# A hybrid encoder block: transfers of V on another queue, another order of the attention minima, and a thinner fourth head pair

## The chip, the cores and the metric

The kernel runs on one core of a Trainium2 chip. The metric is device microseconds of one execution; less is better. Five engines share the work, each with an instruction stream of its own that it takes strictly in order: PE (TensorE, matrix products and transposes), DVE (VectorE), ACT (ScalarE), POOL (GpSimd) and SP (SyncE, which here only issues DMAs). DMAs are also issued from ACT's and POOL's streams. Streams wait for each other by semaphores.

## The reference

One layer over 512 rows of 1024 values, in float32:

```python
h = rms_norm(x, g)
xr, gate, q, k, v = split(h @ w_in)              # 512 each
xr = centred_depthwise_conv(xr)
y_rnn = (rg_lru(xr, forward) + rg_lru(xr, backward)) * gelu(gate)
y_attn = dilated_attention(q, k, v, rel_bias)    # 8 heads of 64
x = x + concat(rms_norm(y_rnn), rms_norm(y_attn)) @ w_out
x = x + square(relu(rms_norm(x) @ w_up)) @ w_down
return rms_norm(x, final_g)
```

The attention has three dilated windows, of which the kernel makes two groups of keys for each block of 128 queries: near ones (within 64 positions, at most 256 keys) and far ones (a multiple of 4 away, hence 128 keys of the same class, position modulo 4).

## The kernel before, in words

Every product is made of three float32r matmuls (`mm3`, L311 to L314): high times high, low times high and high times low part. Weights come in chunks of 128x1024 by DMA into `wraw` (three buffers), or into `tw`, `ws` and `ts` where several blocks are summed first. ACT rounds a chunk to its high part `whi` (`conv_hi`, L260) and DVE subtracts to get the low part `wlo` (`conv_lo`, L268); both happen three chunks ahead of use. After a low part the next `wraw` load is issued on SP's queue (`emit_dma`, L243).

PE, ACT, DVE and POOL run in the order in which the program is written (a manual schedule); for SP the framework chooses the order. So a step's place in the text is its place in each engine's queue.

The part in question runs from 84 to 200 us of the span:

- **V.** ScalarE writes V to the tile `vs` (`v_evac`, L717). Far keys need V sorted by class, so `v_far` (L719 to L722) copies it on-chip into `vc`, the other half of the same tile, by five DMAs on SP's queue. Their first reader is the product of pair 0, in pair 1's turn (`att_av`).
- **The head pairs.** The loop `for i in range(5)`, `for u in range(4)` (L1058) handles heads 2i and 2i+1 together; u is a block of 128 queries. `att_s` (L766) makes the score matmuls: for u = 0 the near scores `pn` of blocks 0 and 1 (L777) and the far scores `pf` of all four (L784), for u = 2 the near scores of blocks 2 and 3. `pn` lies in two PSUM banks that both halves of a pair share. `att_f` (L797) adds the bias to far scores and takes each row's minimum (the scores are negated); `att_e` takes up that minimum, does the same with near scores (L816) and lets ScalarE take the exponential (L819). In the trace a minimum is a custom DVE instruction and a short read of its accumulator, twice, for the two heads.
- One turn later the exponentials are transposed (`att_t`, L831, three groups `a`, `b`, `c` for each head), copied to `ett` by ScalarE, the row factors 1/sum are transposed (`att_r`, L391) and copied to `zrow`, and `att_av` (L912) makes the pair's output `pav`. Transposes, factors and outputs take turns in two PSUM banks (tag `et`), so each needs the copy of the one two before it. DVE multiplies `pav` by `zrow` into `yp` (L928), ScalarE squares it (`ysq`) and scales it (`at`).
- **Fillers.** Between these steps `fill` takes thunks from a queue: first the Q and K projections of the next pairs (48), then the recurrent half of W_out (32 thunks, `pwo`, three matmuls each). `FILL` (L1055) says how many stand at the four places of each (i, u); where it names nothing, one at each. `plan` puts small steps beside them, among them `end(t)` (two DVE products that finish scan t, L570 and L571).
- **W_out's attention half** runs as seven 2x2 block products (Strassen-like, `OSEQ`: 11, s2, s3, s4, 21, s1, 22). The sums of weight blocks s1 to s4 are made by DMA: `load_x` (L992) loads the first block on SP's queue and adds the others on POOL's queue. Each result is added to `x1` by `wo_x` (L1120) with the row factor `rc[1]`: column sums by PE (`col_sums`, L411), mean by DVE (L396), power -1/2 by POOL (L399), and `nrc`, its negative, by DVE (L1147). The next product of the same bank has to wait for that addition.

After 205 us W_up and W_down follow in the same manner, to 530 us, and the final norm.

Of the kernel before, what the change touches and what calls it, by code (L numbers as in the profile page):

```python
# [12 lines left out]
FT = mybir.dt.float32  # L13
FR = mybir.dt.float32r
AF = mybir.ActivationFunctionType
OP = mybir.AluOpType

P = 128
S = 512
# [89 lines left out]
def hybrid_kernel(ctx: ExitStack, tc, xw, xn, w_in, w_v, w_out, w_up, w_dn, gates, vecs, rel, onehot, fg, out):  # L109
    nc = tc.nc  # L110
# [8 lines left out]
    act = nc.scalar.activation  # L119
# [111 lines left out]
    def oblock(b):  # L231
        return w_out[1, int(b[1]) - 1, int(b[0]) - 1]
# [486 lines left out]
    def v_far(j):  # L719
        for a, b, s in (((0, P, 32 * j - 16),) if j else ((0, 64, 112), (64, P, 0))):  # L720
            n = (b - a) // 4
            nc.sync.dma_start(vc[s:s + n], vs[a:b, j, :])  # L722

    last = [scan_ops_end(t) for t in range(4)]

# [266 lines left out]
    def load_x():  # L992
        xb = big.tile([P, KD, S], FT, name="x1", tag="bigA")
        for n in range(2):
            for g in range(4):
                x1[g, n] = xb[:, 2 * g + n, :]
                nc.sync.dma_start(x1[g, n], xn[2 * g + n])
        ws = big.tile([P, 4, 1024], FT, name="ws", tag="bigB")
        for i, (n, bs) in enumerate((("s2", ("11", "12", "22")), ("s3", ("12", "22")), ("s4", ("11", "12", "22", "21")), ("s1", ("11", "12")))):
            t = raws[C_WA + OSEQ.index(n)] = ws[:, i, :]  # L1000
            nc.sync.dma_start(t, oblock(bs[0]))
            for b in bs[1:]:
                nc.gpsimd.dma_start(t, oblock(b), accum_op=OP.add)

    def rnn_end(t):
        last[t]()
# [10 lines left out]
    def end(t):  # L1017
        return lambda: rnn_end(t)

    def sq_(t):  # L1020
        return lambda: rnn_sq(t)
# [4 lines left out]
    def op(fn, *a):  # L1026
        return lambda: fn(*a)


    plan = {(0, 0, 0): [end(0)], (0, 0, 2): [sq_(0), add], (0, 0, 3): [end(1)],  # L1030
            (0, 1, 1): [sq_(1)],
            (0, 2, 3): [add],
            (1, 0, 2): [end(2)],
# [7 lines left out]
    def beside(*key):  # L1041
        for e in plan.pop(key, ()):
            e()
# [5 lines left out]
    for key, fs in (((4, 0, 4), [(o_sum, "s1", 0), (o_sum, "s2", 0), (o_sum, "s3", 0), (o_sum, "s3", 1)]),  # L1049
# [2 lines left out]
                    ((4, 2, 0), [(o_hi, "s3", 0), (o_hi, "s3", 1)]), ((4, 2, 2), [(o_lo, "s3", 0), (o_lo, "s3", 1), (o_sum, "22", 0)]),  # L1052
                    ((4, 2, 4), [(o_hi2, 0)]), ((4, 3, 0), [(o_lo2, 0), (o_hi, "s1", 0)]), ((4, 3, 4), [(o_lo, "s1", 0), (o_hi, "22", 0), (o_lo, "22", 0)])):
        plan[key] = [op(*a) for a in fs]
    FILL = {(3, 1): (1, 1, 1, 0), (3, 2): (1, 1, 1, 0), (3, 3): (1, 1, 1, 0), (4, 0): (0, 1, 0, 0), (4, 1): (0, 1, 0, 1), (4, 2): (0, 1, 0, 0), (4, 3): (0, 0, 0, 1)}  # L1055


    for i in range(5):  # L1058
        for u in range(4):
            if i == 0:  # L1060
                v_far(u)
            if i < 4 and u in (0, 2):
                att_s(i, u)
                if i < 3:
                    load_tw(2 * i + 2 + u // 2)
            if i >= 1 and u < 3:
                att_t(2 * i - 2, "abc"[u])
                att_t(2 * i - 1, "abc"[u])
            if i < 4:
                if u < 2:  # L1070
                    att_f(i, 2 * u)
                    att_f(i, 2 * u + 1)
                att_e(i, u)
            if u == 0 and i >= 1:
                att_z(i - 1)
            beside(i, u, 0)
            fill(FILL.get((i, u), (1, 1, 1, 1))[0])
            beside(i, u, 1)
            fill(FILL.get((i, u), (1, 1, 1, 1))[1])
            if u == 1 and i >= 1:  # L1080
                att_r(i - 1)
            if u == 0 and i >= 2:
                att_y(i - 2)
            beside(i, u, 2)
            fill(FILL.get((i, u), (1, 1, 1, 1))[2])
            beside(i, u, 3)
            fill(FILL.get((i, u), (1, 1, 1, 1))[3])
            beside(i, u, 4)
            if u == 3 and 1 <= i < 4:
                att_av(i - 1)  # L1090
    assert not plan
# [43 lines left out]
    def h2_l(k):  # L1135
        nc.vector.tensor_tensor(hb["l"][:, k, :], hm[k], f(hb["h"])[:, k, :], op=OP.subtract)

    fill(1)
    att_av(3)
    att_y(3)  # L1140
    fill(4)
    cs = col_sums(ssy[1], "gs")
    rc[1] = rstd_cols(cs, S)
    o_sum("s1", 1)
    o_sum("s2", 1)
    nrc = consts.tile([P, 4], FT, name="nrc")
# [563 lines left out]
```

## Time and profile before

| | |
|---|---|
| median of 3 runs | 538.03 us (537.99 to 540.79) |
| the profiled execution | 539.04 us, its span 537.2 us |
| TensorE clock granted | 0.996 |
| PE busy | 524.9 us, 98% of the span |
| DVE, ACT, POOL busy | 423.3, 352.2, 64.0 us |
| DMA | 104.10 MB, 194 GB/s in the mean |

Times inside the profile count from the start of the span. A row of the timeline gives start, duration, engine, line, operation, output and inputs, shape, and in brackets how long the engine had stood idle and what released it. A row of the list of waits gives the total, the count and the longest. A row of the table by stretches gives the stretch, its length, the busy time of PE, PE's weight loads, DVE, ACT and POOL with their instruction counts, the clock, the share of DMA and GB/s. Matmuls are pipelined, so their modelled ends overlap the next starts.

### The profile page before, as it was taken

How to read it: one execution, taken by the hardware profiler on the slowest of the kernel's cores; microseconds unless marked ns; L12 is line 12 of the kernel's file. 1: busy time of each engine (PE TensorE's matmuls, PEld its weight loads, DVE VectorE, ACT ScalarE, POOL GpSimd, SP SyncE). 2: the span in 40 equal slices, each digit the busy share in tenths (PEclk: the TensorE clock that was granted, in tenths of full speed). 3: DMA queues.
4: the chain of work that ended last, by engine and by line, in shares of the span. 5: the costliest groups of instructions: out<-in, count | busy, mean ns of one | idle time of the engine just before them, and what ended most of it. 6: DMA issues, size and time to landing. Idle time of an engine off the chain costs nothing.

```text
span 537.2 us, 9162 instructions
## 1 busy us (share of the span) xinstructions
PE 524.9 (98%) x3507; PEld 448.3 (83%) x3507; DVE 423.3 (79%) x695; ACT 352.2 (66%) x557; POOL 64.0 (12%) x91
## 2 busy tenths in 40 slices
PE   8999999899999999999999999999999999999995
PEld 6866888687887778889999888888999999888884
DVE  6897787776674799889769987879756987987885
ACT  7677957567845745586576755566657686655664
POOL 3330000000001130001030213001001110131000
PEclk9999999999999999999999999999999999999998
DMA  7754068642299688856586799995888496799704
GB/s 276 210 161 141 32 171 182 183 114 70 90 298 307 165 166 203 285 193 180 166 177 177 195 252 274 288 356 116 282 235 206 117 220 193 174 301 263 174 0 157
DMA packets 34587, 104.10 MB, mean 194 GB/s; under 512 B 3981, under 2 KB 6954, under 8 KB 34544
## 3 DMA queue, kind: packets, MB, share of 16 engines
q1 hardware_dynamic: 26304, 74.66, 41.2%
q0 software_dynamic: 7920, 28.61, 28.5%
q8 instruction: 27, 0.44, 0.4%
q10 hardware_dynamic: 320, 0.25, 0.1%
q14 instruction: 16, 0.13, 0.1%
HBM read 96.15 MB, written 4.21 MB: 187 GB/s over the span
## 4 chain that ended last, share of the span: by engine, by line
PE 75%; DMA 10%; ACT 5%; DVE 5%; issue 2%; POOL 1%; SPq 0%; DVEq 0%; ACTq 0%; POOLq 0%
PE pu L314 10%; PE pu L313 10%; PE pu L312 10%; PE pd L312 9%; PE pd L314 9%; PE pd L313 9%; DMA ws<-in_w_out_dram 6%; DMA wraw<-in_w_in_dram 3%; PE pqk L312 2%; PE pqk L313 1%; PE pqk L314 1%; PE pg L502 1%; PE pxr L312 1%; PE pxr L314 1%; PE pxr L313 1%
## 5 line engine op out<-in xcount | busy, mean ns | idle before, releaser
L268 DVE TENSOR_TENSOR wlo<-wraw,whi 128x1024 fp32r<-128x1024 f32 x73 | 88.9, 1221 | 28.3 <-ACT whi L260 28.1
L260 ACT ACTIVATE whi<-wraw 128x1024 fp32r<-128x1024 f32 x70 | 74.0, 1059 | 44.6 <-PE pd L314 20.5
L313 PE MATMUL pd<-wlo,ah 128*128 128x512 f32 (+1 forms) x195 | 75.2, 386 | 0.0
L312 PE MATMUL pd<-whi,ah 128*128 128x512 f32 (+1 forms) x195 | 75.2, 386 | 0.0
L314 PE MATMUL pd<-whi,al 128*128 128x512 f32 (+1 forms) x195 | 75.2, 386 | 0.0
L313 PE MATMUL pu<-hl,whi 128*128 128x256 f32 x224 | 63.4, 283 | 0.0
L314 PE MATMUL pu<-hh,wlo 128*128 128x256 f32 x224 | 63.4, 283 | 0.0
L312 PE MATMUL pu<-hh,whi 128*128 128x256 f32 x224 | 63.4, 283 | 0.0
L260 ACT ACTIVATE whi<-tw 128x1024 fp32r<-128x1024 f32 x36 | 38.1, 1060 | 37.0 <-DMA tw<-in_w_up_dram 10.1
L314 PE MATMUL pu<-h2h,wlo 128*128 128x256 f32 (+1 forms) x200 | 60.1, 301 | 0.2 <-DVE wlo L268 0.2
L312 PE MATMUL pu<-h2h,whi 128*128 128x256 f32 (+1 forms) x200 | 60.1, 300 | 0.0
L313 PE MATMUL pu<-h2l,whi 128*128 128x256 f32 (+1 forms) x200 | 60.0, 300 | 0.0
L268 DVE TENSOR_TENSOR wlo<-tw,whi 128x1024 fp32r<-128x1024 f32 x36 | 44.0, 1222 | 17.5 <-ACT whi L260 17.5
L312 PEld LDWEIGHTS pu<-hh,whi 128*128 128x128 f32 x224 | 43.0, 192 | 0.0
L313 PEld LDWEIGHTS pu<-hl,whi 128*128 128x128 f32 x224 | 43.0, 192 | 0.0
L314 PEld LDWEIGHTS pu<-hh,wlo 128*128 128x128 f32 x224 | 43.0, 192 | 0.0
L314 PEld LDWEIGHTS pd<-whi,al 128*128 128x128 f32 x195 | 36.6, 188 | 7.4
L313 PEld LDWEIGHTS pd<-wlo,ah 128*128 128x128 f32 x195 | 36.6, 188 | 7.4
L312 PEld LDWEIGHTS pd<-whi,ah 128*128 128x128 f32 x195 | 36.6, 188 | 7.2
L260 ACT ACTIVATE whi<-ts 128x1024 fp32r<-128x1024 f32 x24 | 25.5, 1061 | 24.3 <-PE pd L314 18.1
L314 PEld LDWEIGHTS pu<-h2h,wlo 128*128 128x128 f32 x200 | 38.3, 191 | 1.8 <-DVE wlo L268 0.6
L312 PEld LDWEIGHTS pu<-h2h,whi 128*128 128x128 f32 x200 | 38.3, 191 | 1.3
(265 smaller groups left out, 1222.6 us busy)
## 6 DMA issues: line engine op xcount, KB each, us to landing
wraw<-in_w_up_dram SPq DMA_DIRECT2D x25, 512.0 KB
ts<-in_w_dn_dram POOLq DMA_DIRECT2D x24, 512.0 KB, 13.6
wraw<-in_w_dn_dram SPq DMA_DIRECT2D x24, 512.0 KB
tw<-in_w_up_dram SPq DMA_DIRECT2D x15, 512.0 KB
tw<-in_w_up_dram POOLq DMA_DIRECT2D x15, 512.0 KB, 7.4
wraw<-in_w_in_dram SPq DMA_DIRECT2D x13, 512.0 KB
ts<-in_w_dn_dram SPq DMA_DIRECT2D x8, 512.0 KB
tw<-in_w_dn_dram SPq DMA_DIRECT2D x8, 512.0 KB
```

What stands on the lines that cost most here:

```text
L260: act(hi, raws[i], AF.Copy)
L268: nc.vector.tensor_tensor(lo, r, f(splits[i][0]), op=OP.subtract)
L312: nc.tensor.matmul(o, lhsT=a[0], rhs=b[0], start=bool(first), stop=False, skip_group_check=on)
L313: nc.tensor.matmul(o, lhsT=a[0], rhs=b[1], start=False, stop=False, skip_group_check=on)
L314: nc.tensor.matmul(o, lhsT=a[1], rhs=b[0], start=False, stop=bool(last), skip_group_check=on)
L502: nc.tensor.matmul(pg[2 * d + j][halves[b ^ d]], lhsT=gwr[t][halves[b], c], rhs=xc[t][halves[b]], start=True, stop=True)
```

## The change

Five edits:

1. `v_far`'s five DMAs are issued from ScalarE's stream, at the end of each block of pair 0, instead of on SP's queue at its beginning.
2. For block 1 the near minima (`att_e`) come ahead of the far minima of blocks 2 and 3 (`att_f`), and `end(1)` moves from pair 0, block 0, to the step after them.
3. The W_out sums are added in rounds: the second block of each sum, then the third, then the fourth.
4. The last row factor is ScalarE's square root from PSUM and DVE's reciprocal. The square root's table is loaded by a dummy activation after the last exponentials (the last block of pair 3).
5. `FILL`: pair 3 gets two fillers a block (four and three before), the turn after it four in all (five before); after pair 3's product five precede the column sums (four before, with one more ahead of that product), and the rest, nine instead of three, follow them.

```diff
@@ v_far
-            nc.sync.dma_start(vc[s:s + n], vs[a:b, j, :])
+            nc.scalar.dma_start(vc[s:s + n], vs[a:b, j, :])
@@ load_x
-        for i, (n, bs) in enumerate((("s2", ("11", "12", "22")), ("s3", ("12", "22")), ("s4", ("11", "12", "22", "21")), ("s1", ("11", "12")))):
-            t = raws[C_WA + OSEQ.index(n)] = ws[:, i, :]
-            nc.sync.dma_start(t, oblock(bs[0]))
-            for b in bs[1:]:
-                nc.gpsimd.dma_start(t, oblock(b), accum_op=OP.add)
+        sums = (("s2", ("11", "12", "22")), ("s3", ("12", "22")), ("s4", ("11", "12", "22", "21")), ("s1", ("11", "12")))
+        for i, (n, bs) in enumerate(sums):
+            raws[C_WA + OSEQ.index(n)] = ws[:, i, :]
+            nc.sync.dma_start(ws[:, i, :], oblock(bs[0]))
+        for m in (1, 2, 3):
+            for i, (n, bs) in enumerate(sums):
+                if m < len(bs):
+                    nc.gpsimd.dma_start(ws[:, i, :], oblock(bs[m]), accum_op=OP.add)
@@ plan
-    plan = {(0, 0, 0): [end(0)], (0, 0, 2): [sq_(0), add], (0, 0, 3): [end(1)],
+    plan = {(0, 0, 0): [end(0)], (0, 0, 2): [sq_(0), add], (0, 1, 0): [end(1)],
@@ FILL
-    FILL = {(3, 1): (1, 1, 1, 0), (3, 2): (1, 1, 1, 0), (3, 3): (1, 1, 1, 0), (4, 0): (0, 1, 0, 0), (4, 1): (0, 1, 0, 1), (4, 2): (0, 1, 0, 0), (4, 3): (0, 0, 0, 1)}
+    FILL = {(3, u): (0, 1, 1, 0) for u in range(4)}
+    FILL.update({(4, 0): (0, 1, 0, 0), (4, 1): (0, 1, 0, 0), (4, 2): (0, 1, 0, 1), (4, 3): (0, 0, 0, 0)})
@@ the loop over pairs
-            if i == 0:
-                v_far(u)
...
-                if u < 2:
-                    att_f(i, 2 * u)
-                    att_f(i, 2 * u + 1)
+                if u == 0:
+                    att_f(i, 0)
+                    att_f(i, 1)
                 att_e(i, u)
+                if u == 1:
+                    att_f(i, 2)
+                    att_f(i, 3)
+                if (i, u) == (3, 3):
+                    act(warm, epsb, AF.Sqrt)
...
             beside(i, u, 4)
+            if i == 0:
+                v_far(u)
@@ after the loop
-    fill(1)
     att_av(3)
     att_y(3)
-    fill(4)
+    fill(5)
     cs = col_sums(ssy[1], "gs")
-    rc[1] = rstd_cols(cs, S)
+    rc[1] = consts.tile([P, 4], FT, name="rc1")
+    act(rc[1], cs, AF.Sqrt, scale=1.0 / S, bias=epsb)
+    nc.vector.reciprocal(rc[1], rc[1])
```

What this does to the queues is seen at three places. First, DVE in pair 0, block 1: L816 are the near minima, L797 and L801 the far ones with their cleared gaps, L570 and L571 the end of scan 1.

```order
 L571 TENSOR_TENSOR gt<-gt,ga 128x512
 L753 SCALAR_TENSOR_TENSOR kraw<-pqk,rrow 128x512
+L816 ISA e,mn<-pn,tw,mf 128x256
+L816 ISA mn 128x1
+L816 ISA e,mn<-pn,tw,mf 128x256
+L816 ISA mn 128x1
+L797 ISA e,mf<-pf,tw 128x128
```

The near minima now come directly behind pair 1's K. This is where they stood, behind all four far minima and the end of scan 1, with a weight split after them:

```order
-L801 MEMSET e 128x64
-L797 ISA e,mf<-pf,tw 128x128
-L797 ISA mf 128x1
-L801 MEMSET e 128x64
-L816 ISA e,mn<-pn,tw,mf 128x256
-L816 ISA mn 128x1
-L816 ISA e,mn<-pn,tw,mf 128x256
-L816 ISA mn 128x1
 L268 TENSOR_TENSOR wlo<-wraw,whi 128x1024
```

The far minima and the end of scan 1 now stand between the near minima and that split. The other pairs change in the same way, without the scan.

Second, PE in the turn after pair 3, after the transposed row factors (`prow`), ahead of the last group of transposes (`pt`):

```order
 L391 MATMUL prow<-ident,rzb 128x128 x4
-L312 MATMUL pwo<-whi,yh 128x512
-L313 MATMUL pwo<-wlo,yh 128x512
-L314 MATMUL pwo<-whi,yl 128x512
 L831 MATMUL pt<-ident,e 128x128 x8
-L312 MATMUL pwo<-whi,yh 128x512
-L313 MATMUL pwo<-wlo,yh 128x512
-L314 MATMUL pwo<-whi,yl 128x512
```

The filler that stood between the two is gone, and one of those behind them.

Third, DVE from pair 3's output `yp` to the first additions of W_out's attention half (L1120); `rv`, `rcol` and `nrc` belong to the row factor, L967 adds the recurrent half's results. Before:

```order
L928 TENSOR_TENSOR yp<-pav,zrow 128x4x4x32
L588 TENSOR_TENSOR ysq<-ysq 128x512
L967 SCALAR_TENSOR_TENSOR x_1705<-pwo,rcol_1579,x_1705 128x512
L268 TENSOR_TENSOR wlo<-ws,whi 128x1024
L967 SCALAR_TENSOR_TENSOR x_1705<-pwo,rcol_1579,x_1705 128x512
L396 TENSOR_SCALAR rv<-pcs 128x4
L891 TENSOR_TENSOR osum<-at 128x256
L893 SCALAR_TENSOR_TENSOR osum<-at,osum 128x256
L1147 TENSOR_SCALAR nrc<-rcol_2199 128x4
L967 SCALAR_TENSOR_TENSOR x_1705<-pwo,rcol_1579,x_1705 128x512 x2
L875 TENSOR_TENSOR ol<-osum,oh 128x256
L1120 SCALAR_TENSOR_TENSOR x_1705<-pwo,rcol_2199,x_1705 128x512 x2
```

Now, from the reciprocal on (L1120 has become L1129):

```order
L1153 RECIPROCAL rc_2172<-rc_2172 128x4
L891 TENSOR_TENSOR osum<-at 128x256
L893 SCALAR_TENSOR_TENSOR osum<-at,osum 128x256
L1157 TENSOR_SCALAR nrc<-rc_2172 128x4
L268 TENSOR_TENSOR wlo<-ws,whi 128x1024
L967 SCALAR_TENSOR_TENSOR x_1705<-pwo,rcol_1579,x_1705 128x512
L268 TENSOR_TENSOR wlo<-ws,whi 128x1024
L967 SCALAR_TENSOR_TENSOR x_1705<-pwo,rcol_1579,x_1705 128x512 x3
L875 TENSOR_TENSOR ol<-osum,oh 128x256
L1129 SCALAR_TENSOR_TENSOR x_1705<-pwo,rc_2172,x_1705 128x512 x2
```

The row factor has moved ahead of two weight splits and all four additions of the recurrent half's second column block.

## The prediction

> **What bounds the kernel now.** First the page's line of busy times, then PE's list of waits between 90 and 200 us, the stretch in which every edit lies.
>
> ```profile
> PE 524.9 (98%) x3507; PEld 448.3 (83%) x3507; DVE 423.3 (79%) x695; ACT 352.2 (66%) x557; POOL 64.0 (12%) x91
> ...
> PE pn L777 <- DVE mn L816: 1.3, 1, 1.3
> PE pwo L312 <- DVE x L1120: 1.0, 2, 0.6
> PE pt L831 <- DVE rz L842: 0.7, 1, 0.7
> PE pt L831 <- ACT ett L833: 0.4, 1, 0.4
> PE pn L777 <- DVE qraw L749: 0.2, 1, 0.2
> PE pcs L411 <- DVE ysq L588: 0.2, 1, 0.2
> ```
>
> PE is busy for 98% of the span, and the change takes no matmul away. It can only win or lose in the seven short gaps of this list, 3.8 us together. Every other term must be hidden behind PE, or it costs. A gap is priced below from start to start against the same sequence without a wait, since a wait also stretches the matmuls beside it. "Old clock" means the times of this profile. A "pass" is the three matmuls of one weight chunk on one 128-row block.
>
> **Part 1: near minima first, and the end of scan 1 behind them.** PE at the end of block 0 of pair 0, then the same step in pair 1, where nothing waits:
>
> ```profile
> 104.74 0.39 PE L312 MATMUL pqk<-h_hi,whi 128*128 128x512 f32 x1
> ...
> 105.19 0.39 PE L314 MATMUL pqk<-h_hi,wlo 128*128 128x512 f32 x1
> 106.92 1.39 PE L777 MATMUL pn<-kraw,qraw 64*32 64x256 f32 x32 [1.34 <-DVE mn L816]
> 108.24 0.50 PE L312 MATMUL pqk<-h_hi,whi 128*128 128x512 f32 x1
> ...
> 123.29 0.40 PE L314 MATMUL pqk<-h_hi,wlo 128*128 128x512 f32 x1
> 123.61 0.99 PE L777 MATMUL pn<-kraw,qraw 64*32 64x256 f32 x32
> 124.53 0.66 PE L831 MATMUL pt<-ident,e 128*128 128x128 f32 x4
> ```
>
> From the last projection matmul past the scores takes 108.24 - 105.19 = 3.05 us with the wait and 124.53 - 123.29 = 1.24 without: the gap costs 1.81 us. (104.74 to 105.19 is two matmuls, 0.225 each, so a pass takes 0.68.) VectorE at that time:
>
> ```profile
> 104.10 0.68 DVE L570 TENSOR_TENSOR ga<-ga,hs 128x512 f32<-128x512 f32 x1
> ...
> 105.42 0.28 DVE L797 CUSTOM_DVE_ANT_0 e<-pf,tw 128x128 f32<-128x128 f32 x1
> ...
> 106.35 0.41 DVE L816 CUSTOM_DVE_ANT_0 e<-pn,tw,mf 128x256 f32<-128x256 f32 x1
> ...
> 107.10 1.22 DVE L268 TENSOR_TENSOR wlo<-wraw,whi 128x1024 fp32r<-128x1024 f32 x1
> ```
>
> The scores need the banks that the near minima read, and those end at 107.10. Ahead of them stand the end of scan 1 (104.10 to 105.42, 1.32 us) and four far minima (105.42 to 106.35, 0.93 us). Both go behind, so the minima end at 107.10 - 2.25 = 104.85, before PE asks at about 105.4. Gain **1.81 us**. The work moved is not gone: far minima, scan end and weight split then end where they ended before, and the next near minima follow at their old place; the first to need them is the score step of pair 1, eight passes or 5.5 us later. I keep 0 as the low end (the wait reappears there).
>
> **Part 2: ScalarE issues the class transfers.**
>
> ```profile
> SPq L722 <- ACT vs L717: 7.7, 3, 3.8
> ...
> 85.58 1.74 SPq L722 DMA_DIRECT2D vs<-vs  x2
> 87.44 0.52 SPq L243 DMA_DIRECT2D wraw<-in_w_in_dram  x1
> ...
> 94.53 1.06 ACT L260 ACTIVATE whi<-wraw 128x1024 fp32r<-128x1024 f32 x1 [1.21 <-DMA wraw<-in_w_in_dram]
> ...
> 95.63 1.23 DVE L268 TENSOR_TENSOR wlo<-wraw,whi 128x1024 fp32r<-128x1024 f32 x1 [3.89 <-ACT whi L260]
> ```
>
> SP waits 7.7 us in three places to issue transfers whose source ScalarE is still writing, and a weight load stands right behind two of them. That load is split at 94.53, 1.21 us late; the low part follows at 95.63, `qraw` stands behind it on VectorE, and PE waits the 0.2 of the list's fifth row. Without the transfers the load can leave up to 1.9 us sooner (87.44 - 85.58), so the **0.2 us** goes. The Trainium skill, "DMA: Bandwidth & Descriptors", section "Issuing engines are not separate DMA queues", says that issuing from several engines saves only the sequencer's time of issue. By that alone this term would be 0 and the sum 0.2 smaller; the 7.7 us of SP waits say that here an in-order queue is held, which is another matter.
> The five issues cost ScalarE time: 1.74 us for two on SP, about 0.6 each after that, so some 3 us over pair 0, between exponentials. The first reader of those exponentials is the transposition in pair 1, and that of the transfers comes later still. I take 0; low end -0.5, one issue that holds ScalarE for a landing (the fourth and fifth wait for the first two to land).
>
> **Part 3: fourth pair thinned.** Passes before pair 3's product go from 19 to 12; the column sums then have five passes ahead instead of four, and nine behind instead of three. Engines in the two stretches, up to pair 2's product and up to pair 3's:
>
> ```profile
> 154.65:169.68 15.03, 15.03 (x197) 12.02 (x195) 9.39 (x43) 9.31 (x24) 2.68 (x3) 1.00 1.05 330
> 169.68:181.36 11.68, 10.60 (x80) 8.01 (x79) 5.94 (x13) 8.53 (x18) 0.87 (x1) 1.00 0.90 238
> 177.20 0.60 PE L391 MATMUL prow<-ident,rzb 128*128 128x128 f32 x4
> ...
> 177.56 0.47 PE L312 MATMUL pwo<-whi,yh 128*128 128x512 f32 x1
> ...
> 177.84 0.60 ACT L851 ACTIVATE zrow<-prow 128x512 f32<-128x512 f32 x1 [0.17 <-PE prow L391]
> ...
> 521.92 1.28 ACT L1356 ACT_TABLE_LOAD   x1
> ```
>
> PE's part shrinks to 15.03 - 5 x 0.68 = 11.6 us beside 9.4 of VectorE and 9.3 of ScalarE, and to 11.68 - 2 x 0.68 = 10.3 beside 8.5 of ScalarE: neither becomes the bound by sum, but covers get short. One breaks on paper. After the transposed row factors (177.20) a pass stood ahead of the last transpositions; now none does. Their second half needs the bank that the copy `zrow` reads, which ends at 178.44, 1.24 us after the row's start. Four transposes move PE on by 0.36 (177.20 to 177.56), so row and first half take 0.72. Loss **0.5**; ends 0 and 1.1 (a late copy, 0.60 more). The waits of 0.7 and 0.4 lie at pair 3's first transpositions, which keep their one pass: unchanged. The new table load (1.28) stands behind the last exponentials and under pair 2's product: 0, and up to 1.3 without that cover. The 0.2 at the column sums goes with the fifth pass: **0.2**.
>
> **Part 4: last row factor by square root.**
>
> ```profile
> 190.13 1.15 POOL L399 TENSOR_TENSOR rcol<-rv,mhalf 128x4 f32<-128x4 f32 x1 [4.06 <-DVE rv L396]
> ...
> 191.31 0.17 DVE L1147 TENSOR_SCALAR nrc<-rcol 128x4 f32<-128x4 f32 x1 [0.47 <-POOL rcol L399]
> 191.39 1.41 DVE L967 SCALAR_TENSOR_TENSOR x<-pwo,rcol,x 128x512 f32<-128x512 f32 x2
> ...
> 193.04 1.40 DVE L1120 SCALAR_TENSOR_TENSOR x<-pwo,rcol,x 128x512 f32<-128x512 f32 x2
> 194.36 1.21 DVE L268 TENSOR_TENSOR wlo<-ws,whi 128x1024 fp32r<-128x1024 f32 x1
> ...
> 196.43 0.74 DVE L1120 SCALAR_TENSOR_TENSOR x<-pwo,nrc,x 128x512 f32<-128x512 f32 x1
> ...
> 190.35 0.39 PE L312 MATMUL pwo<-whi,oh 128*128 128x512 f32 x1
> ...
> 193.84 0.50 PE L312 MATMUL pwo<-whi,oh 128*128 128x512 f32 x1 [0.60 <-DVE x L1120]
> ...
> 197.23 0.50 PE L312 MATMUL pwo<-whi,oh 128*128 128x512 f32 x1 [0.38 <-DVE x L1120]
> ```
>
> VectorE stands until 191.31 for GpSimd's power, and the results behind it come late: `11` is added from 193.04, so `s2` starts at 193.84, not after four passes at 190.35 + 2.73 = 193.1. With nine passes of cover the factor is early. Then `11`'s first half is added as its passes end (191.75), its second by 193.8, and `s2` runs 193.1 to 195.9, losing 0.1. But a weight split, a split and a sum (194.36 to 196.43, 2.07 us) still follow: `s2`'s own result ends at 193.8 + 2.1 + 0.7 = 196.6. `s3` starts there instead of at 197.23. Gain **0.6**; ends 0 and 1.4 (eight passes from 190.35 end at 195.8: both gaps gone).
>
> **Part 5: sums round robin.**
>
> ```profile
> 162.24 2.68 POOL L1003 DMA_DIRECT2D ws<-in_w_out_dram  x3 [9.66 <-DMA ws<-in_w_out_dram]
> ...
> DMA to landing us min/median/max: 5.4/8.8/14.5
> ```
>
> GpSimd no longer stands behind one sum's landing before it starts the next. But `s2`, needed first, gets its last add behind three others, about 165 instead of 162.24; at the longest landing that is 179.5. ScalarE wants it at about 182: 0.
>
> **The sum.** 1.81 + 0.2 + 0.2 + 0.6 - 0.5 = 2.3 us. After 200 PE hardly waits and loads leave as buffers come free, so it should carry to the end. Against the profiled execution: 539.04 (span 537.2 and 1.84 around it) - 2.3 = 536.7. The median shown is 538.03, 1.01 lower: **535.7 us**.
>
> **The rivals.**
> - *Every gap touched goes.* No loss at `zrow`, and both gaps at `pwo` vanish (1.4 start to start): 1.81 + 0.2 + 0.2 + 1.4 = 3.6, so 534.4. For it: short waits often fall into slack. Against it: VectorE's 2.07 us before `s2`'s result. Chance 0.17.
> - *The thinned pair gives it back.* ScalarE's copies come late at three places, 0.60 each: 2.3 - 1.8 = 0.5, so 537.5. For it: ScalarE at 8.5 of 10.3 us. Chance 0.15.
> - *VectorE is the bound in pair 0.* Then the change does not do there what it says: the 1.81 returns at pair 1's scores, 537.5. Against it: the projection passes between. Chance 0.10.
> - *`s2` lands late: slower.* Five adds then share what three shared: 14.5 x 5 / 3 = 24 us, landing at 189. ScalarE's split of `s2` stands ahead of the square root, which VectorE waits for with two weight splits and four results behind it, 5 us of work due by 190.35. Landings after 183.6 cost in full: 5.4 late, 3.1 net, 541.1. It decides from 186 on. Against it: the median landing of 8.8. Chance 0.08.
>
> **How the numbers follow.** The forecast has 0.50, and its own range is 534.8 to 536.6, a little over half the way to the ends of its terms. 0.5% of 538.03, about what a measurement of this kernel can tell from no change, is 2.7 us: faster means below 535.3. A third of the forecast (0.17) and the first rival (0.17) lie there: faster 0.34. The rest of the forecast and the two that end at 537.5 give same 0.58; slower is 0.08. The range runs from the first rival less 0.4 to the 537.5 cases plus 0.5: 534.0 to 538.0. It leaves out the slow rival and tails.
>
> **What would show it.** Right: no gap at pair 0's second scores, weight splits ahead of `qraw` earlier, a gap of about half a microsecond before pair 3's last transpositions, `s3` of W_out waiting some 0.7 us while `s2` waits hardly at all, and no GpSimd power before it. Wrong: PE waiting at pair 1's scores, ScalarE idle at a transfer's landing between 105 and 115, or VectorE waiting for ScalarE's square root behind the copy of `s2`.

## The result, and the profile after

The changed kernel takes 536.18 us (median of 7 runs, 535.86 to 536.6), the kernel before in the same comparison 538.91 (7 runs, 537.74 to 541.51). The ratio is 0.9945, with a 95% interval of 0.9922 to 0.9968: faster beyond doubt, by 0.55%. Whether that passes the 0.5% that the prediction took as its line stays open: the interval takes 0.995 in, and the time itself is not below the 535.3 us that it named. Forecast were 535.7 us and a difference of 2.3. In the three sets of experiments below (11 to 31 runs each) the kernel before has medians of 538.33 to 538.52; against those the difference is 2.2 to 2.3, or 0.4%. The profiled run of the changed kernel has 536.6 us and a span of 534.7, 2.5 less than before.

The page's line of busy times, then PE's list of waits between 90 and 200 us, both of the changed kernel:

```profile
PE 524.5 (98%) x3507; PEld 448.4 (84%) x3507; DVE 423.6 (79%) x695; ACT 352.1 (66%) x559; POOL 62.3 (12%) x90
...
PE pt L831 <- DVE rz L842: 0.7, 1, 0.7
PE pwo L312 <- DVE x L1129: 0.7, 2, 0.5
PE pt L831 <- ACT ett L833: 0.4, 1, 0.4
PE pt L831 <- ACT zrow L851: 0.2, 1, 0.2
```

PE's work is the same, and where seven gaps stood there are five. Those at the scores (1.3 and 0.2) and at the column sums (0.2) are gone, one at `zrow` (0.2) is new, and the two at pair 3's first transpositions stand as they were.

PE at both scores of pair 0, from the last projection matmul past the scores of block 1:

```profile
97.75 0.39 PE L314 MATMUL pqk<-h_hi,wlo 128*128 128x512 f32 x1
98.07 0.99 PE L777 MATMUL pn<-kraw,qraw 64*32 64x192 f32 x32
...
105.28 0.39 PE L314 MATMUL pqk<-h_hi,wlo 128*128 128x512 f32 x1
105.60 0.99 PE L777 MATMUL pn<-kraw,qraw 64*32 64x256 f32 x32
106.52 0.50 PE L312 MATMUL pqk<-h_hi,whi 128*128 128x512 f32 x1
```

106.52 - 105.28 = 1.24 us where it was 3.05: the 1.81 of the prediction, to the hundredth. VectorE shows the order that does it:

```profile
102.91 0.68 DVE L753 SCALAR_TENSOR_TENSOR kraw<-pqk,rrow 128x512 f32<-128x512 f32 x1
103.51 0.48 DVE L816 CUSTOM_DVE_ANT_0 e<-pn,tw,mf 128x256 f32<-128x256 f32 x1
...
104.32 0.29 DVE L797 CUSTOM_DVE_ANT_0 e<-pf,tw 128x128 f32<-128x128 f32 x1
...
105.25 0.63 DVE L570 TENSOR_TENSOR ga<-ga,hs 128x512 f32<-128x512 f32 x1
...
106.53 1.22 DVE L268 TENSOR_TENSOR wlo<-wraw,whi 128x1024 fp32r<-128x1024 f32 x1
```

The near minima begin right behind pair 1's K and end at about 104.3, 1.3 us before PE wants their banks; far minima, scan end and weight split follow.

The class transfers, on ScalarE's queue (ACTq), beside ScalarE's own work:

```profile
103.20 0.68 ACTq L722 DMA_DIRECT2D vs<-vs  x1
103.57 1.04 ACT L260 ACTIVATE whi<-wraw 128x1024 fp32r<-128x1024 f32 x1
103.92 0.60 ACTq L722 DMA_DIRECT2D vs<-vs  x1
104.56 0.62 ACT L819 ACTIVATE e<-e,mn 128x384 f32<-128x384 f32 x1
```

The issue of 103.92 lies inside an activation that runs from 103.57 to 104.61 and keeps its usual length. The stream goes on to the exponential with no idle time: the transfers cost ScalarE nothing that shows.

PE in the turn after pair 3, and at the start of the last stage:

```profile
172.06 0.60 PE L391 MATMUL prow<-ident,rzb 128*128 128x128 f32 x4
172.49 0.60 PE L831 MATMUL pt<-ident,e 128*128 128x128 f32 x4
173.34 0.66 PE L831 MATMUL pt<-ident,e 128*128 128x128 f32 x4 [0.25 <-ACT zrow L851]
...
188.72 0.39 PE L312 MATMUL pwo<-whi,oh 128*128 128x512 f32 x1
...
192.44 0.50 PE L312 MATMUL pwo<-whi,oh 128*128 128x512 f32 x1 [0.17 <-DVE x L1129]
...
195.26 0.47 PE L312 MATMUL pwo<-whi,oh 128*128 128x512 f32 x1 [0.49 <-DVE x L1129]
```

The first half of the last transpositions starts 0.43 after the row factors, the second half 0.85 after the first: a loss of 0.42. From the first product of the last stage to `s3` it takes 195.26 - 188.72 = 6.54 us; before it was 197.23 - 190.35 = 6.88.

Against the record of before, PE's steps change by -0.31 at the first scores (1.10 us for 1.41), -1.90 at the second (the 1.81 and 0.09 of stretch), +0.09 from there to the last stage and -0.34 in it: -2.46 together. Two differences that no edit touches come on top and cancel. PE reaches the first scores 0.49 later in this record, nearly all of it from the first load of the program. And the last store is issued at 533.16 before and at 531.14 now, with 4.0 and 3.6 us from there to the end of the span (537.2 and 534.7).

### The profile page after: what moved, and what is told of

It is laid out like the page before. It is cut to its first block, busy times and chain, and to the rows that moved or that the text cites. A ratio compares the mean times of both kernels' runs of the same rounds, so it can differ in the third digit from the quotient of the medians.

```text
span 534.7 us, 9167 instructions
## 1 busy us (share of the span) xinstructions
PE 524.5 (98%) x3507; PEld 448.4 (84%) x3507; DVE 423.6 (79%) x695; ACT 352.1 (66%) x559; POOL 62.3 (12%) x90
## 4 chain that ended last, share of the span: by engine, by line
PE 92%; DMA 3%; DVE 2%; ACT 1%; issue 1%; SPq 0%; DVEq 0%; ACTq 0%
PE pu L314 10%; PE pu L313 10%; PE pu L312 10%; PE pd L313 9%; PE pd L312 9%; PE pd L314 9%; PE pqk L312 3%; PE pqk L314 3%; PE pqk L313 3%; PE pav L912 2%; PE pt L831 2%; DMA wraw<-in_w_up_dram 2%; PE pg L502 2%; PE pwo L312 2%; PE pv L312 2%; PE pwo L314 2%
## 5 line engine op out<-in xcount | busy, mean ns | idle before, releaser
L313 PEld LDWEIGHTS pu<-h2l,whi 128*128 128x128 f32 x200 | 38.3, 191 | 1.3
```

What stands on the lines that cost most here:

```text
L313: nc.tensor.matmul(o, lhsT=a[0], rhs=b[1], start=False, stop=False, skip_group_check=on)
```

## The experiments

Twelve variants were timed, in three sets of four, each set on another chip and with its own runs of the kernel before. "Below" and "above" are against that kernel's median in the same set. The changed kernel ran in none of these sets; where a variant is compared with its 536.18, the difference is good to a few tenths at best.

| run | what it is | median us | before | ratio (95%) |
|---|---|---|---|---|
| b_near | before + part 1 | 537.03 | 538.35 | 0.9977 (0.9967 to 0.9987) |
| b_vfar | before + part 2 | 537.80 | 538.35 | 0.9993 (0.9985 to 1.0002) |
| b_root | before + part 4 | 537.68 | 538.35 | 0.9994 (0.9984 to 1.0004) |
| b_thin | before + part 3 | 538.31 | 538.35 | 0.9998 (0.9989 to 1.0006) |
| b_end | before + the scan's end alone | 537.15 | 538.52 | 0.9968 (0.9954 to 0.9982) |
| a_vsync | changed, without part 2 | 536.45 | 538.52 | 0.9958 (0.9946 to 0.9970) |
| a_unthin | changed, without part 3 | 539.52 | 538.52 | 1.0016 (1.0007 to 1.0025) |
| imp | changed, passes at the gaps | 535.83 | 538.52 | 0.9941 (0.9929 to 0.9954) |
| b_robin | before + part 5 | 541.18 | 538.33 | 1.0051 (1.0038 to 1.0065) |
| a_serial | changed, without part 5 | 536.36 | 538.33 | 0.9963 (0.9949 to 0.9978) |
| b_core | before + parts 1, 2, 4 | 536.24 | 538.33 | 0.9957 (0.9943 to 0.9971) |
| imp2 | imp, two orders mended | 535.70 | 538.33 | 0.9946 (0.9933 to 0.9960) |

The theory going in: the order on VectorE in pair 0 brings most of the gain, the rest is small. The rivals: a sum of small things; GpSimd's power, with the spread of the runs of before for evidence.

### The order in pair 0: b_near and b_end

b_near:

```diff
-... (0, 0, 3): [end(1)],
+... (0, 1, 0): [end(1)],
...
-                if u < 2:
-                    att_f(i, 2 * u)
-                    att_f(i, 2 * u + 1)
+                if u == 0:
+                    att_f(i, 0)
+                    att_f(i, 1)
                 att_e(i, u)
+                if u == 1:
+                    att_f(i, 2)
+                    att_f(i, 3)
```

> The kernel before with only the near minima of each pair's second block put ahead of its third and fourth blocks' far minima, and the end of scan 1 moved behind them; class transfers, fills, sums and row factor as before. My theory: this order is three quarters of the gain, 1.8 us below before, no wait at pair 0's second scores (1.24 us from the last projection matmul past the scores, instead of 3.05), and all other gaps as before: qraw 0.2, pwo 0.6 and 0.4, column sums 0.2. Rival (the gain is the sum of small things, and the scan's end comes back as a wait further on): under 1.0 us below before, with a new wait at pair 1's scores or at a weight split. Rival (GpSimd's power sets the end): 0 to 0.5 below before, and the spread of the times stays as wide as before's, 537.7 to 541.5.

b_end has the first two lines of that diff alone.

> The kernel before with only the end of scan 1 moved behind pair 0's second-block near minima; the far minima stay ahead of the near ones. In three records of code that is the same up to there, the second scores of pair 0 took 3.05, 2.89 and 2.37 us from the last projection matmul past them, against 1.24 without a wait. The scan's end is 1.32 us of VectorE. My theory (two things add up there: VectorE's order, and how late the weight load lands that is split ahead of the minima): 1.24 to 1.75 us from start to start, and 0.9 to 1.3 us below before. Rival (the minima's order is what counts, the scan's end only follows): 2 us or more from start to start, under 0.5 us below before.

b_near came out 1.3 us below before, b_end 1.4: the order is the largest share, but less than the 1.8 of the record, and in times the scan's end alone does as much as both moves. The second scores in b_near, b_end and b_root (whose code is that of before up to there), from the projection matmul past the scores:

```profile
104.54 0.39 PE L314 MATMUL pqk<-h_hi,wlo 128*128 128x512 f32 x1
104.86 0.99 PE L777 MATMUL pn<-kraw,qraw 64*32 64x256 f32 x32
105.77 0.50 PE L312 MATMUL pqk<-h_hi,whi 128*128 128x512 f32 x1
```

```profile
104.41 0.39 PE L314 MATMUL pqk<-h_hi,wlo 128*128 128x512 f32 x1
104.73 1.38 PE L777 MATMUL pn<-kraw,qraw 64*32 64x256 f32 x32
106.04 0.50 PE L312 MATMUL pqk<-h_hi,whi 128*128 128x512 f32 x1
```

```profile
104.62 0.39 PE L314 MATMUL pqk<-h_hi,wlo 128*128 128x512 f32 x1
105.67 1.39 PE L777 MATMUL pn<-kraw,qraw 64*32 64x256 f32 x32 [0.66 <-DVE mn L816]
106.99 0.50 PE L312 MATMUL pqk<-h_hi,whi 128*128 128x512 f32 x1
```

1.23 us without a gap, 1.63 with the scan's end moved alone (in a record whose load was late, by the measure below: split at 97.50, first scores at 97.10), 2.37 in the order of before. So two things follow. The scan's end carries most: b_end keeps 0.39 of the gap, and by the prediction's rows that is 107.10 - 1.32 = 105.78 against 105.4. In b_end the list of waits shows nothing there at all; the 0.39 is only in the stretched scores (1.38 for 0.99). And the gap is no constant: with the same code it took 3.05, 2.89, 2.45 and 2.37 in four records (before, b_thin, b_robin, b_root). What differs is when the second weight half is split, from before and from b_root:

```profile
98.38 1.06 ACT L260 ACTIVATE whi<-wraw 128x1024 fp32r<-128x1024 f32 x1 [2.27 <-DMA wraw<-in_w_in_dram]
```

```profile
97.08 1.06 ACT L260 ACTIVATE whi<-wraw 128x1024 fp32r<-128x1024 f32 x1 [2.23 <-DMA wraw<-in_w_in_dram]
```

Both wait for the load. The low part and the far minima stand behind that split on VectorE, so the minima are late by as much as the load is. The first scores come at 97.89 and 97.41, so the split is 0.49 behind them in the one and 0.33 ahead in the other: 0.82 apart, of which 0.68 reach the second scores. The other two records lie between: in b_thin the split is 0.24 behind (97.63 against 97.39), in b_robin 0.20 ahead (97.67 against 97.87). The record of before was on the late side (539.04 us, where 31 runs had a median of 538.35). The rivals fall: no new wait appears at pair 1's scores, and the spread of b_near's times (536.49 to 538.21) is that of before in its set (537.57 to 539.28).

### The transfers: b_vfar and a_vsync

b_vfar (and, the other way round, a_vsync):

```diff
-            nc.sync.dma_start(vc[s:s + n], vs[a:b, j, :])
+            nc.scalar.dma_start(vc[s:s + n], vs[a:b, j, :])
...
-            if i == 0:
-                v_far(u)
...
             beside(i, u, 4)
+            if i == 0:
+                v_far(u)
```

> The kernel before with only the class transfers issued by ScalarE, after each step's passes instead of ahead of the step on SP. My theory: 0.2 to 0.3 us below before, since the weight load leaves SP some 1.7 us sooner, its split follows, and the wait for qraw at pair 0's first scores (0.2) goes; the wait at the second scores stays at 1.3. By the Trainium skill, DMA: Bandwidth & Descriptors, section Issuing engines are not separate DMA queues, taken alone: 0. Rival (ScalarE pays for the issues, five at about 0.6): 0.5 to 1 us above before, with VectorE or PE waiting for an exponential or for the split of a weight in pair 0.

> The changed kernel with the class transfers back on SP, ahead of the steps, as before. My theory: the second scores stay without a wait, since the near minima now have 0.7 to 1.3 us in hand there, and only the wait for qraw at the first scores can come back (0.31 from start to start in the record of before, 0 in three others): 0 to 0.3 us above the changed kernel, so some 1.9 to 2.2 below before. Rival (the transfers and the order each need the other): 0.7 us or more above the changed kernel, with a wait for minima at the second scores. Rival (ScalarE paid for the issues): below the changed kernel.

In b_vfar the loads leave early, ScalarE's second split stands at 94.31 instead of 98.38 and waits for nothing. The gap at the first scores is gone, and the second scores take 2.38 us, as in the records whose load came in time:

```profile
94.31 1.05 ACT L260 ACTIVATE whi<-wraw 128x1024 fp32r<-128x1024 f32 x1
```

```profile
105.42 0.39 PE L314 MATMUL pqk<-h_hi,wlo 128*128 128x512 f32 x1
106.48 1.39 PE L777 MATMUL pn<-kraw,qraw 64*32 64x256 f32 x32 [0.67 <-DVE mn L816]
107.80 0.50 PE L312 MATMUL pqk<-h_hi,whi 128*128 128x512 f32 x1
```

The load behind that split leaves SP in this order, before and in b_vfar (the first of the three loads that each row takes together):

```profile
89.99 7.22 SPq L243 DMA_DIRECT2D wraw<-in_w_in_dram  x3
```

```profile
88.71 6.78 SPq L243 DMA_DIRECT2D wraw<-in_w_in_dram  x3
```

It leaves 1.28 us sooner, while the split comes 4.07 sooner. The rest is the transfer itself: before, it took 8.4 us from issue to split, in b_vfar at most 5.6. In the records whose class transfers are on SP it took 7.0 (b_root) to 8.4, so most of what differs between them is the landing and not the queue. Whether the class transfers, moved beside the load, slow it, no run here shows.

So parts 1 and 2 cured one wait from two ends. That wait's order share is 2.38 - 1.24 = 1.14 us, its load share 0 to 0.7, depending on the run. With the new order the load has slack, and a_vsync lies 0.3 above the changed kernel's median, with no wait at either score. The interval of b_vfar takes in 1: in times the part cannot be told from nothing.

### Row factor and thinning: b_root, b_thin, a_unthin

b_root:

```diff
+            if (i, u) == (3, 3):
+                act(warm, epsb, AF.Sqrt)
...
-    rc[1] = rstd_cols(cs, S)
+    rc[1] = consts.tile([P, 4], FT, name="rc1")
+    act(rc[1], cs, AF.Sqrt, scale=1.0 / S, bias=epsb)
+    nc.vector.reciprocal(rc[1], rc[1])
```

> The kernel before with only the last row factor made by square root and reciprocal, and the square root's table loaded behind pair 3's last exponentials; the passes and the sums stay as before, so three passes lie behind the column sums. My theory: the factor comes some 1.9 us earlier, the wait of 0.6 ahead of s2's product goes, that ahead of s3's stays or grows, because VectorE's split of weights, low part and sum stand ahead of s2's result: 0.6 us below before. Rival (GpSimd's power, behind its accumulating transfers in an in-order queue, sets the end in most runs): 1.5 to 2 us below before, and runs as close together as those after the change (0.8 us) instead of 3.8. Rival (three passes are too few, and the change needs its nine): within 0.2 of before.

b_thin (and, the other way round, a_unthin):

```diff
-    FILL = {(3, 1): (1, 1, 1, 0), (3, 2): (1, 1, 1, 0), (3, 3): (1, 1, 1, 0), (4, 0): (0, 1, 0, 0), (4, 1): (0, 1, 0, 1), (4, 2): (0, 1, 0, 0), (4, 3): (0, 0, 0, 1)}
+    FILL = {(3, u): (0, 1, 1, 0) for u in range(4)}
+    FILL.update({(4, 0): (0, 1, 0, 0), (4, 1): (0, 1, 0, 0), (4, 2): (0, 1, 0, 1), (4, 3): (0, 0, 0, 0)})
...
-    fill(1)
     att_av(3)
     att_y(3)
-    fill(4)
+    fill(5)
```

> The kernel before with only the new fills: twelve passes instead of nineteen ahead of pair 3's product, five instead of four ahead of the column sums, nine instead of three behind them; the row factor stays GpSimd's power. My theory: the wait ahead of pair 3's last transpositions appears (0.25 shown, 0.4 from start to start), that at the column sums goes (0.2), and the nine passes cover the power, so that the wait ahead of s2's product goes and that ahead of s3's stays: 0.3 to 0.6 us below before. Rival (the passes were only moved, the power's wait with them): within 0.2 of before or up to 0.4 above it.

> The changed kernel with the passes of pair 3 where they were before (nineteen ahead of its product, four ahead of the column sums, three behind them); order, transfers, sums and square root as changed. My theory: thinning gave nothing back: the wait ahead of pair 3's last transpositions goes (0.4 from start to start), that at the column sums returns (0.2), and s3 comes 6.46 us after the first product of the last stage, as with the square root alone, instead of 6.54: 0.2 to 0.3 us below the changed kernel, some 2.4 below before. Rival (the square root needs the nine passes): 0.4 us or more above the changed kernel, with a wait for the row factor ahead of s2's product.

b_root's PE at the start of the last stage:

```profile
189.06 0.39 PE L312 MATMUL pwo<-whi,oh 128*128 128x512 f32 x1
...
191.99 0.50 PE L312 MATMUL pwo<-whi,oh 128*128 128x512 f32 x1
...
195.52 0.50 PE L312 MATMUL pwo<-whi,oh 128*128 128x512 f32 x1 [0.40 <-DVE x L1122]
```

The wait ahead of `s2` is gone and `s3` comes after 6.46 us: a gain of 0.42 with only three passes behind the column sums. The nine passes do not improve on that (6.54). In times b_root cannot be told from before, and b_thin changed nothing that can be measured, where 0.3 to 0.6 us were expected: its nine passes do not cover GpSimd's power. VectorE stands 2.24 us for it, until 187.07, with two weight splits and four results behind, and both waits of the last stage stay (0.44 and 0.43).

a_unthin was the surprise. Expected 0.2 to 0.3 us below the changed kernel, it came 3.3 above, and slower than before in its own set. The rival that had a loss in store had it at the row factor; there is none. The wait is elsewhere, at pair 3's product. ScalarE's stream and then PE's:

```profile
180.24 1.06 ACT L260 ACTIVATE whi<-ws 128x1024 fp32r<-128x1024 f32 x1 [3.47 <-DMA ws<-in_w_out_dram]
181.20 1.06 ACT L833 ACTIVATE ett<-pt 128x512 f32<-128x512 f32 x2
```

```profile
181.83 4.43 PE L912 MATMUL pav<-ett,vs 128*64 128x128 f32 x32 [2.67 <-ACT ett L833]
```

ScalarE waits 3.47 us for `s2`'s sum to land, with the copies of pair 3's last transpositions queued behind its split, and the product waits for the copies.

### The sums: b_robin, a_serial and b_core

b_robin (and, the other way round, a_serial):

```diff
-        for i, (n, bs) in enumerate((("s2", ("11", "12", "22")), ("s3", ("12", "22")), ("s4", ("11", "12", "22", "21")), ("s1", ("11", "12")))):
-            t = raws[C_WA + OSEQ.index(n)] = ws[:, i, :]
-            nc.sync.dma_start(t, oblock(bs[0]))
-            for b in bs[1:]:
-                nc.gpsimd.dma_start(t, oblock(b), accum_op=OP.add)
+        sums = (("s2", ("11", "12", "22")), ("s3", ("12", "22")), ("s4", ("11", "12", "22", "21")), ("s1", ("11", "12")))
+        for i, (n, bs) in enumerate(sums):
+            raws[C_WA + OSEQ.index(n)] = ws[:, i, :]
+            nc.sync.dma_start(ws[:, i, :], oblock(bs[0]))
+        for m in (1, 2, 3):
+            for i, (n, bs) in enumerate(sums):
+                if m < len(bs):
+                    nc.gpsimd.dma_start(ws[:, i, :], oblock(bs[m]), accum_op=OP.add)
```

> The kernel before with only W_out's sums issued round robin. Theory from the run without thinning: with the passes where they were, ScalarE's split of s2 stands ahead of the copies of pair 3's last transpositions, and round robin lets s2 land some 2 to 3 us later, so that PE waits for the copies ahead of pair 3's product: 1.5 to 3 us above before, with a wait of 1.5 to 3 for ett at that product. Rival (round robin alone costs nothing, and what cost the run without thinning was the square root's table or ScalarE's class transfers): within 0.4 us of before.

> The changed kernel with W_out's sums one after the other, as before; thinned pair, order, transfers and square root as changed. Theory (thinning moves ScalarE's split of s2 behind pair 3's copies, and round robin only uses that room): within 0.3 us of the changed kernel, ScalarE waiting some 4 us for s4's last add as there. Rival (round robin pays by itself, for s3 or s4 would land too late in a row): 0.6 us or more above the changed kernel, with a new wait of PE in the last stage.

b_core is before with the diffs of b_near, b_vfar and b_root.

> The kernel before with three of the five parts: near minima first and the scan's end behind them, class transfers on ScalarE, last row factor by square root; passes and sums as before. Theory (thinning and round robin cancel each other): 1.7 to 2.2 us below before, so within 0.4 us of the changed kernel, with the waits 0.7, 0.4, 0.2 (column sums) and 0.4 (ahead of s3) left. Rival (the thinned pair carries a share of its own, 0.5 us or more): under 1.7 us below before. Rival (the three parts overlap, since order and transfers cure one wait): under 1.4 us below.

Round robin alone costs 2.9 us. ScalarE's stream in before, in b_robin and in the changed kernel, around the split of `s2`:

```profile
178.94 1.05 ACT L260 ACTIVATE whi<-ws 128x1024 fp32r<-128x1024 f32 x1
179.89 1.07 ACT L833 ACTIVATE ett<-pt 128x512 f32<-128x512 f32 x2
```

```profile
180.90 1.06 ACT L260 ACTIVATE whi<-ws 128x1024 fp32r<-128x1024 f32 x1 [2.58 <-DMA ws<-in_w_out_dram]
181.86 1.06 ACT L833 ACTIVATE ett<-pt 128x512 f32<-128x512 f32 x2
```

```profile
180.54 1.04 ACT L260 ACTIVATE whi<-ws 128x1024 fp32r<-128x1024 f32 x1
182.63 0.26 ACT L1152 ACTIVATE rc<-pcs,epsb 128x4 f32<-128x4 f32 x1 [1.04 <-PE pcs L411]
```

Before, the split runs at 178.94 without a wait, ahead of the copies (`ett`). With round robin `s2` lands at 180.9. In the changed kernel fewer passes have gone by, and the split hangs on one of them; it comes behind pair 3's output, where nothing for pair 3 is queued behind it, and finds `s2` there. It starts at 180.54 without idle time ahead of it. In the two runs where ScalarE waited, the landing was at 180.2 and 180.9, which is 16.0 and 15.7 us after the issue of `s2`'s last add. In the changed kernel that issue is at 164.05 (the second of two from 163.16, 1.78 us together); an estimate from these durations puts the landing at 179.7 to 180.0, and the margin at 0.5 to 0.8 us.

The list shows less than such a wait costs. PE at pair 3's product in b_robin, then the table by stretches (the third number from the end is the granted clock) for the product in b_robin, in a_unthin and in before:

```profile
182.50 4.96 PE L912 MATMUL pav<-ett,vs 128*64 128x128 f32 x32 [1.78 <-ACT ett L833]
```

```profile
183.00:186.00 3.00, 3.00 (x21) 2.46 (x23) 2.73 (x5) 1.78 (x5) 0.88 (x1) 0.50 0.05 12
```

```profile
182.00:184.00 2.00, 2.00 (x17) 1.80 (x19) 1.40 (x4) 1.97 (x6) 0.53 (x1) 0.50 0.03 8
```

```profile
181.00:184.00 3.00, 3.00 (x34) 1.94 (x33) 2.69 (x5) 1.82 (x5) 0.00 (x0) 1.00 0.63 122
```

Behind the waits of 1.78 and 2.67 us the granted clock is half for about 3.4 us, and the product takes 4.96 and 4.43 us where it took 2.82. From the start of pair 3's last transpositions to the column sums PE takes 12.67 us in b_robin and 12.99 in a_unthin, 8.96 before: 3.7 and 4.0 more, for 1.8 and 2.7 in the list.

So thinning is what lets round robin pass, and round robin brings nothing that can be measured: a_serial is 0.2 us from the changed kernel, and b_core, with neither, has its time (536.24 and 536.18). One thing expected of a_serial did not come: its ScalarE does not wait for `s4`'s last add. In the changed kernel it does, for 4.18 us, and PE does not feel it. GpSimd's power as the cause of the spread falls too: b_root, without it, spread from 536.95 to 539.81.

### A version with the gaps covered: imp and imp2

imp:

```diff
-... (4, 1): (0, 1, 0, 0), ...
+... (4, 1): (0, 1, 0, 1), ...
...
                 att_av(i - 1)
+                if i == 3:
+                    fill(2)
...
-    fill(5)
+    fill(4)
...
-    BES["s2"].update({1: lambda: (o_lo2(1), o_sum("22", 1)), 2: lambda: o_hi("s1", 1)})
+    BES["s2"].update({2: lambda: (o_lo2(1), o_sum("22", 1), o_hi("s1", 1))})
```

> The changed kernel with passes put where PE still waits: two behind pair 2's product (ahead of pair 3's first transpositions), one between the transposed row factors and pair 3's last transpositions, four instead of five ahead of the column sums and seven instead of nine behind them; and in the last stage s2's first result ahead of the low part and the sum for later products (1.06 us of VectorE). My theory: each wait is short cover and nothing else, so that the 0.7 and 0.4 at pair 3's first transpositions, the 0.2 at its last ones and the 0.5 ahead of s3 go: 1.5 to 1.9 us below the changed kernel, some 4 below before. Rival (the waits move on: less cover behind the column sums lets the row factor or s2's split come late): within 0.5 us of the changed kernel, with a new wait of 0.5 or more ahead of the last stage's products.

imp2, on top of imp (`lo4` is the weight split that stood at this place):

```diff
-                if b in (1, 17, 21, 25):
-                    conv_hi(C_WO + {1: 3, 17: 4, ...
+                if b in (1, 18, 21, 25):
+                    conv_hi(C_WO + {1: 3, 18: 4, ...
...
-    BES["s2"].update({2: lambda: (o_lo2(1), o_sum("22", 1), o_hi("s1", 1))})
+    BES["s2"].update({2: lambda: o_hi("s1", 1), 3: lambda: (o_lo2(1), o_sum("22", 1), lo4())})
```

> The changed kernel with the passes of the run imp, W_out's first weight split one pass later, behind the copy of pair 3's transposed row factors, and both of s2's results ahead of the low part and the sum for later products. Theory (short cover, in the order in which the results are wanted): no wait longer than 0.1 us between pair 3's first transpositions and s4's product, 0.5 to 0.8 us below imp and 1.2 to 2 below the changed kernel, so 3 to 4 below before. Rival (the waits move on to s4's product or to the column sums): no faster than imp.

In imp the gaps at pair 3's first transpositions are gone. That at `zrow` stayed: a weight split now stood ahead of the copy on ScalarE. imp2 moves that split, and the list of waits between 90 and 200 us has one row left:

```profile
PE pwo L312 <- DVE x L1131: 0.7, 2, 0.4
```

The wait ahead of `s3` is 0.26 there, and a new one of 0.42 stands ahead of `s4`, behind VectorE's next weight split. PE's last matmul starts 1.04 us earlier than in the changed kernel's record (527.23 and 528.27), where the first projections start within 0.02 us of each other. The span is only 0.2 us shorter, since the last store took 4.4 us to the end of it instead of 3.6. The times show less than PE's gain too: 535.83 and 535.70, each against 536.18 in another set, with intervals that overlap. Both beat the kernel before; that they beat the changed one is likely by the records and not shown by the times. Below the changed kernel, imp was to gain 1.5 to 1.9 us and came to 0.35; imp2 was to gain 1.2 to 2 and came to 0.5. Both lie where their rivals had them, and in imp2 the wait moved on, as its rival said.

## Why the prediction was right, point by point

- **The sum.** 2.3 us forecast; 2.2 to 2.7 measured, 2.5 by the steps of PE. That it came out owes something to luck: alone, the five parts come to 1.3, 0.6, 0.7, 0.0 and -2.9 us, together -0.3. The chance of "faster" (0.34) was low for a forecast that lay 0.4 us from its line.
- **Part 1** had the mechanism, the place and the arithmetic: 1.81 in these two records, and b_end's 0.39 from the same rows. The step that failed is to take one record's gap as the gap: as part of the kernel the order is worth 1.1 to 1.8, and 1.3 in times. The rest of the 1.81 was the late load that part 2 cures, which the sum has booked under part 1.
- **Part 2**: 0.2 forecast, 0.31 in the record, and ScalarE paid nothing, as said. That SP's queue was held is in the rows, but less by the waits than by the issues. The low part that frees the buffer of the load at 87.44 ends at 85.20 (in b_vfar the same load leaves 0.03 us behind it); of the 2.24 us until that load leaves, 0.38 are the wait for ScalarE's V and 1.74 the two issues. The Trainium skill, "DMA: Bandwidth & Descriptors", section "Issuing engines are not separate DMA queues", says that issuing from several engines saves only the sequencer's time of issue, which is usually small. That saving is what the rows show here, so the prediction was wrong to set its 7.7 us of SP waits against the rule; its term of 0 by that rule is allowed as well by the interval of b_vfar, 0.9985 to 1.0002. What the part is worth stays open: 0 to 0.8 us by that interval without part 1, and with it some 0.3, not told from nothing.
- **Part 3**: the loss at `zrow` was 0.42 for 0.5, and the 0.2 at the column sums went. But the part was priced as if thinning only moved cover. It also moves what hangs on the passes, and ScalarE's split of `s2` is one of these.
- **Part 4**: 0.34 for 0.6 (0.42 by itself). The 2.07 us of VectorE ahead of `s2`'s result were right (192.30 to 194.37). That result was put at 0.7 behind them, where it took 0.9 until PE started (194.37 to 195.26), and the second result of `11` came 0.1 later than I had it. "With nine passes of cover the factor is early" was needless: three are enough.
- **Part 5** failed as a step, with a sum that came out: "ScalarE wants it at about 182: 0". The landing was put a little early (at most 179.5, measured 180.2 and 180.9). The want was read for the new order alone. In the old order the split is wanted at some 178, with pair 3's copies behind it, and there the same landing costs 2.9 us. A third to a half of what PE loses there (1.3 of 4.0 us in a_unthin, 1.9 of 3.7 in b_robin) comes behind the wait, at the lower clock, which no term of the prediction has. Part 5 costs that without part 3, and part 3 takes the cost away; I had added up each against the kernel before. That both were in the change is luck of the forecast, not its doing.
- **The rivals.** "`s2` lands late" had the engine and the transfer, but put the harm at the square root, the landing at 189 and the point of decision at 186. It landed at 180.2 and 180.9 (four adds follow one another there, not five), and the changed kernel decides at some 180.5, so 0.08 was low for a case so near. Its size (3.1 us; 2.9 in b_robin, 3.3 between a_unthin and the changed kernel) agreed by luck. VectorE as the bound in pair 0 did not come: nothing waits at pair 1's scores. Neither did all gaps go.

What stays open: how often `s2`'s landing passes 180.5 in the changed kernel (its seven runs, within 0.8 us of each other, show no such case), why the load ahead of the second scores takes 7.0 us in one record and 8.4 in another, and how the ends of the program spread from run to run: in the fourteen records PE's first projection on a whole weight chunk starts between 7.44 and 8.63, and from the last store's issue to the end of the span it takes 3.5 to 4.4 us.

## What to carry to other kernels

A wait in one record is one draw: before pricing its removal, look at which row released it, and whether that row itself waited for a transfer. Where an edit thins or moves filler work, list what is hooked to the fillers (splits, issues, copies), find where it lands on each in-order engine, and ask what is queued behind it that others wait for; two edits that look free or harmful alone may exist for each other. Then test each part both ways, alone and taken out: thinning alone showed nothing here, and only taken out did it show what it is for. And read the granted clock behind a long wait before taking the listed idle time as its price.

## What the runs showed of the hardware

In the changed kernel's trace, the view of the tile of W_out's sums has this line on GpSimd's transfers:

```profile
DMA to landing us min/median/max: 6.7/10.0/16.2
```

- A DMA issue on ScalarE's queue (0.56 to 0.68 us) ran inside activations and did not lengthen them; on SP two such issues took 1.74 us of the queue, ahead of a weight load.
- Accumulating transfers landed 6.7 to 16.2 us after issue in this record, and 5.4 to 14.5 before. The longest is 15.7 to 16.3 in the six records with round robin and 14.2 to 15.1 in the eight without: 0.6 to 2.1 more, not the factor of 5 / 3 that the rival had taken.
- Behind idle times of PE of 1.78 and 2.67 us its granted clock was 0.50 for about 3.4 us. Behind shorter ones, up to the 1.34 at pair 0's second scores, it stayed at 1.00; in the changed kernel's record no stretch of 4 us ahead of the last matmul is below 0.995.
- A wait of the list can hide in stretched matmuls: in b_end no wait is listed, yet the scores take 1.38 us instead of 0.99 and the step 0.39 longer.
